# The output products of a state space, two groups of 64 rows in turn, in a hybrid decoder layer

## The chip, the cores and the metric

The kernel runs on one core of one Trainium2 chip. The metric is the device time of one execution in microseconds, lower is better. Times of a kernel are medians of several executions; profiles are of one execution. The engines are named PE (matrix products, with PEld for its weight loads), DVE, ACT, POOL and SP (which issues DMA).

## The reference

One decoder layer over 2048 positions of width 1024, in float32. After an RMSNorm one projection feeds two token mixers: differential attention (4 heads, two softmax maps each) and a diagonal state space of 32 channel groups with 16 channels and 64 complex states each. Both outputs go through one output projection; then come a second RMSNorm, a gated FFN of width 2816, and a last RMSNorm. The part that matters here:

```python
def s5_mixer(u, lam_re, lam_im, log_step, b_re, b_im, c_re, c_im, d, w_glu, b_glu):
    ...
    _, _, x_re, x_im = lax.associative_scan(combine, (a_re, a_im, bu_re, bu_im), axis=1)
    y = (jnp.einsum('ghp,bsgp->bsgh', c_re.astype(f32), x_re)
         - jnp.einsum('ghp,bsgp->bsgh', c_im.astype(f32), x_im)
         + d.astype(f32) * u32)
    y = jax.nn.gelu(y.reshape(bsz, s_len, SSM_WIDTH))
    y = y * jax.nn.sigmoid(y @ w_glu.astype(f32) + b_glu.astype(f32))
    return y.astype(u.dtype)
```

## The kernel before

All matrix products take float32 values split in two parts, a high one and the rest, so each product is three on PE (`mm3`: high by high, high by rest, rest by high).

**The state space** runs in `ssm_pair`, once for each of 16 pairs of channel groups. Positions are cut in 256 blocks of 8. For a pair n the kernel
- loads the inputs u (128 rows for each group), G, H, and every second time T;
- computes the drive z of the states, 6 products of 128 rows by 256 columns into the PSUM tile `pv1` (pv in the profile);
- starts the outputs y with the products of T by u, 3 for each group: group 0 into `fx1` (fx), group 1 into `tp2[1]` (tp);
- copies z to SBUF on ACT, turns and scans it on DVE and POOL, turns it back and splits it into `xh` and `xl`;
- adds the products of H by the states onto the same y. H and the states hold group 0 in rows 0 to 63 and group 1 in rows 64 to 127, so these products have 64 rows. For each group there are 2 halves f of the states by 3 products, 6 in all, 128 by 256 outputs each;
- applies GELU to fx and tp on ACT into `gy` and stores it to `yD`.

In the profile, the products of 64 rows are those of the form `64*128 64x256`, and `pair` is the PSUM of the projections that run between.

**The order of work.** Nothing is issued as it is written. `Rec` records each operation as a task with a cost from a table, and the operands it reads and writes; `Sched` then simulates the engines and writes out an order for each engine's queue, taking of the ready tasks the one with the best priority (`pri`). Operations marked `any` go to DVE or POOL by the plan. Several matrix products in a row become one task: `Rec.call` collects them in `self.open`, and `flush` closes the task, when asked, when the next product writes another PSUM tile, or when the sum of costs passes 1.3. So the six products of group 0 were one task and those of group 1 another, with a `flush` behind each, and the planner could put other work between them. State space tasks have priority -50, and projections of queries, keys and values (-40 and later) fill PE between them. On the chip each engine runs its queue in the planner's order, waiting on semaphores.

**Behind the state space** the last queries and keys (q0, k0) are rotated: ACT copies the projection out of PSUM, PE multiplies it with a permutation (`tp<-misc,cst`), DVE and POOL combine it with cosine and sine, ACT and DVE split it, and SP stores it. It uses buffers of the state space (the tags tr, t1, t2, pq), so it starts when the last pair is done. Then come the last value projections, and `glu`, the gate: it loads `w_glu` in two parts (L1473), splits them (L1479 on ACT, L1480 on DVE or POOL), loads `yD` (L1486), splits it (L1493, L1496), and multiplies (L518 to L520 into fx). The two loads share a ring of three buffers. Attention's score products (L1199) and exponentials (L1237) follow, then output projection and FFN.

Of the kernel before, what the change touches and what calls it, by code (L numbers as in the profile page):

```python
# [167 lines left out]
class Ring:  # L168


    def __init__(self, *tiles):
        self.free = [(0.0, t) for t in tiles]
        self.queues = {}
# [123 lines left out]
class Rec:  # L297


    def __init__(self, S, nc):  # L300
        self.S, self.real, self.pri, self.mem, self.open = S, nc, 0.0, {}, []
        self.areas, self.turned, self.fair = {}, {}, False
        for name, eng in (("vector", "dve"), ("scalar", "act"), ("gpsimd", "pool"), ("tensor", "pe"), ("sync", "sp"),
                          ("any", "any")):
            setattr(self, name, Proxy(self, name, eng))
# [67 lines left out]
    def urgent(self, pri):  # L373
# [4 lines left out]
        self.flush()  # L378
        self.pri = old

    def flush(self):
        if self.open:
            calls, self.open = self.open, []
            self.last = self.task(("pe", sum(c[0] for c in calls)), [("", *c[1:]) for c in calls])

    @staticmethod
    def isap(x):
        return hasattr(x, "tensor") and hasattr(x, "ap")

    def call(self, eng, f, args, kw):  # L390
        isap = self.isap
        outs = [kw[n] for n in ("out", "accum_out") if isap(kw.get(n))]
        rest = [x for n, x in kw.items() if n not in ("out", "accum_out") and isap(x)]
        pos = [x for x in args if isap(x)]
        if "out" not in kw:
            outs.append(pos.pop(0))
        ins = rest + pos
        free = lambda x: math.prod(n for _, n in list(x.ap)[1:])
        n = max([free(outs[0])] + ([free(i) for i in ins] if "reduce" in f else []))
        c = ("", f, outs, ins, args, kw)  # L400
        if eng == "pe":
            cost = n / 2400.0 + 0.0035
            if f == "transpose":
                cost = 0.108
            elif kw["rhs"].dtype == F32:
                cost = max(4 * cost, 0.215)
            if self.open and (sum(x[0] for x in self.open) + cost > 1.3
                              or kw.get("start") and self.where(self.open[-1][2][0]) != self.where(outs[0])
                              or self.open[-1][2][0].tensor.name != outs[0].tensor.name):
                self.flush()  # L410
            self.open.append((cost, f, outs, ins, args, kw))
            return None
        self.flush()
        if f == "dma_start":
            return self.task(("sp", 0.47), [c], size=math.prod(outs[0].shape) * 4)
        psum = [x.space == PSUM for x in (outs[0], *ins)]
        if f == "tensor_tensor_scan" or psum[0]:
            dve = 2.3e-3 * n + 0.03
        elif f in ("tensor_scalar", "memset"):
            dve = 0.75e-3 * n + 0.03  # L420
        else:
            dve = 1.06e-3 * n + 0.06 if any(psum) else 1.27e-3 * n + 0.02
        cost = dict(dve=dve, act=0.87e-3 * n + (0.26 if "accum_out" in kw else 0.08),
                    pool=(1.0e-3 if f == "tensor_scalar" else 0.3e-3 if f == "memset" else 2.0e-3) * n + 0.12)
        if kw.get("op") == ALU.pow:
            cost["pool"] += 0.25 + 0.09 * n
        port = f == "tensor_tensor" and not any(psum)
        if eng == "any":
            return self.task({e: cost[e] for e in ("dve", "pool")}, [c], bias=FAIR if self.fair else BIAS, port=port)
        return self.task((eng, cost[eng]), [c], port=port)  # L430
# [14 lines left out]
def view(t, shape, dt):  # L445

    if dt != F32:
        t = t.bitcast(dt)
    if len(shape) > 2:
        names = "abcdef"[:len(shape) - 1]  # L450
        t = t.rearrange(f"p ({' '.join(names)}) -> p {' '.join(names)}", **dict(zip(names, shape[1:])))
    return t
# [47 lines left out]
class K:  # L500
# [519 lines left out]
    def ssm_pair(self, n):  # L1020

        nc = self.nc
# [8 lines left out]
        G, H = (s3.tile([128, 2, 2, 128], F32R, name="s" + x) for x in "GH")  # L1031
# [33 lines left out]
        y = [z[:, 0:256] for z in (self.fx1, self.tp2[1])]  # L1065
# [6 lines left out]
        lo, hi = slice(0, 64), slice(64, 128)  # L1072
# [10 lines left out]
        r = self.r8[:, n:n + 1].to_broadcast([128, 256])  # L1083
# [9 lines left out]
        v.tensor_tensor(out=t1[:, 1], in0=t1[:, 1], in1=t2[:, 0], op=ALU.add)  # L1093
        xh, xl = (s1.tile(P3, F32R, name=x) for x in ("xh", "xl"))
        self.split(xh[:, :, 1:], xl[:, :, 1:], t1[:, :, 0:255])
        for g in range(2):
            r = slice(64 * g, 64 * g + 64)
            for f in range(2):

                x = f ^ g  # L1100
                self.mm3(y[g], H[r, f, 0], H[r, f, 1], xh[r, x], xl[r, x], False, f == 1, skip_group_check=True)
            nc.flush()
        gy = view(self.gy, P3, F32)
        for g in range(2):
            a_.activation(out=gy[:, g], in_=y[g], func=AF.Gelu_apprx_tanh)
# [1088 lines left out]
```

## Time and profile before

| | |
|---|---|
| Median of three runs | 2430.85 us (2430.6 to 2438.7) |
| The profiled execution | 2428.99 us |
| Its span | 2426.9 us |
| Busy on DVE, ACT, POOL | 67%, 43%, 43% of the span |
| Mean granted clock of PE | 0.985 |
| Moved by DMA | 435.34 MB |

The profile is read from the time of each engine in total to the stages. The work of the state space's pairs lies between 233 and 406 us, the rest of the rotation and of the value projections until about 480 us, attention until about 1150 us, and the FFN fills the rest. In rows of the timeline, the first number is the start in us, the second the time from the first start to the last end, and `x3` says how many instructions were merged; matrix products are pipelined, so the spacing of their starts counts, not their length. Brackets at a row's end give how long the engine sat idle before it, and what ended that.

### The profile page before, as it was taken

What the parts mean: (1) busy time and instruction counts of PE and PEld (TensorE: products, weight loads), DVE (VectorE), ACT (ScalarE), POOL (GpSimd) and SP (SyncE); (2) the same over time, 40 slices, a digit from 0 to 9 for tenths busy, and PEclk for the clock granted to TensorE, in tenths of its full rate; (3) what the DMA queues carried; (4) which work ended last, traced back from release to release, by engine and by line L of the source; (5) the groups of instructions that cost most, each with busy time, mean ns of one, the idle gap of its engine ahead of it and who ended that gap; (6) DMA issues with size and microseconds to landing.
All of it is one profiled execution on the core that took longest, in us unless ns stands there. A gap on an engine that the chain in (4) does not pass through costs nothing.

```text
span 2426.9 us, 34139 instructions
## 1 busy us (share of the span) xinstructions
PE 2335.0 (96%) x11832; PEld 1958.1 (81%) x11832; DVE 1616.7 (67%) x2577; ACT 1048.9 (43%) x2103; POOL 1041.0 (43%) x1048
## 2 busy tenths in 40 slices
PE   7999999989999999998999999999999999999998
PEld 6887797878888888876788888788888878878876
DVE  7885775247887778647877455754544576585698
ACT  7222333247877776545332333533333342242343
POOL 4134675355666556546544322222232223232244
PEclk9999999999999999998999999999999999999999
DMA  6467675665566557787886232532223255575664
GB/s 216 132 191 215 225 220 170 208 215 156 191 199 193 191 187 245 232 294 234 270 285 223 74 97 81 187 109 78 87 72 96 84 165 198 171 256 165 201 201 162
DMA packets 312174, 435.34 MB, mean 179 GB/s; under 512 B 42241, under 2 KB 187713, under 8 KB 312001
## 3 DMA queue, kind: packets, MB, share of 16 engines
q1 hardware_dynamic: 309408, 428.71, 55.4%
q10 hardware_dynamic: 2592, 4.45, 0.5%
q8 instruction: 93, 1.52, 0.3%
q14 instruction: 81, 0.66, 0.1%
HBM read 287.66 MB, written 145.42 MB: 178 GB/s over the span
## 4 chain that ended last, share of the span: by engine, by line
PE 70%; DMA 6%; DVE 4%; issue 3%; POOL 2%; ACT 2%; SPq 0%; POOLq 0%; DVEq 0%; ACTq 0%
PE pair L519 9%; PE pair L520 9%; PE pair L518 9%; PE tp L519 4%; PE tp L520 4%; PE tp L518 4%; PE fx L518 4%; PE fx L519 3%; PE fx L520 3%; PE pv L518 3%; PE pv L519 3%; PE pv L520 3%; PE pair L364 3%; DMA hn<-qD 2%; PE tp L1320 2%
## 5 line engine op out<-in xcount | busy, mean ns | idle before, releaser
L1782 ACT CAST misc<-hn 128x512 fp32r<-128x512 f32 (+1 forms) x340 | 204.8, 609 | 484.2 <-POOL hn L1902 163.0
L519 PE MATMUL pair<-hn,misc 128*128 128x512 f32 x925 | 363.4, 393 | 10.0 <-DVE hn L1783 9.9
L518 PE MATMUL pair<-hn,misc 128*128 128x512 f32 x925 | 362.2, 392 | 0.5 <-ACT misc L1782 0.4
L520 PE MATMUL pair<-hn,misc 128*128 128x512 f32 x925 | 361.9, 391 | 0.2 <-DVE misc L1783 0.2
L1783 DVE TENSOR_TENSOR misc<-hn,misc 128x512 fp32r<-128x512 f32 (+1 forms) x340 | 247.8, 732 | 113.7 <-ACT misc L1782 113.3
L364 PE MATMUL pair<-hn,misc 128*128 128x512 f32 x1152 | 282.8, 399 | 0.0
L364 PEld LDWEIGHTS pair<-hn,misc 128*128 128x128 f32 x1152 | 215.3, 191 | 45.7 <-issue 2.4
L1902 POOL TENSOR_TENSOR hn<-misc,hn 128x512 f32<-128x512 f32 (+1 forms) x68 | 99.9, 1469 | 296.5 <-DVE misc L1783 296.0
L519 PEld LDWEIGHTS pair<-hn,misc 128*128 128x128 f32 x925 | 174.6, 189 | 51.1 <-DVE hn L1783 15.6
L1909 POOL TENSOR_TENSOR hn<-hn 128x512 f32<-128x512 f32 (+1 forms) x68 | 97.1, 1428 | 256.7 <-DVE misc L1783 240.3
L518 PEld LDWEIGHTS pair<-hn,misc 128*128 128x128 f32 x925 | 174.4, 189 | 38.5 <-ACT misc L1782 0.8
L520 PEld LDWEIGHTS pair<-hn,misc 128*128 128x128 f32 x925 | 174.8, 189 | 36.5 <-DVE misc L1783 0.6
L1899 POOL TENSOR_TENSOR misc<-hn 128x512 f32<-128x512 f32 (+1 forms) x68 | 92.9, 1366 | 245.8 <-DVE misc L1783 200.1
L1221 DVE TENSOR_REDUCE small<-pair 128x1 f32<-128x1024 f32 (+7 forms) x160 | 158.2, 992 | 57.3 <-PE pair L1203 27.0
L1237 ACT ACTIVATE hn<-pair,small 128x1024 f32<-128x1024 f32 (+4 forms) x192 | 166.2, 868 | 60.1 <-DVE small L1221 27.1
L519 PE MATMUL tp<-hn,misc 128*128 128x512 f32 x454 | 177.6, 391 | 3.9 <-DVE hn L1783 3.9
L518 PE MATMUL tp<-hn,misc 128*128 128x512 f32 x454 | 177.4, 391 | 2.1 <-ACT misc L1782 1.9
L520 PE MATMUL tp<-hn,misc 128*128 128x512 f32 x454 | 177.2, 390 | 0.0
L364 POOL TENSOR_TENSOR misc<-misc,misc 128x512 f32<-128x512 f32 (+1 forms) x71 | 84.4, 1190 | 162.8 <-DVE misc L364 130.2
L1946 DVE TENSOR_TENSOR misc<-pair,misc 128x512 f32<-128x512 f32 x110 | 75.9, 690 | 95.9 <-PE pair L520 95.6
L364 POOL TENSOR_TENSOR misc<-misc 128x256 f32<-128x256 f32 (+1 forms) x128 | 102.2, 809 | 44.3 <-DVE misc L364 20.0
L364 DVE TENSOR_TENSOR misc<-misc,misc 128x512 f32<-128x512 f32 (+7 forms) x111 | 93.9, 864 | 36.5 <-ACT misc L364 30.5
(268 smaller groups left out, 5724.5 us busy)
## 6 DMA issues: line engine op xcount, KB each, us to landing
hn<-vD SPq DMA_DIRECT2D x48, 512.0 KB
hn<-kD SPq DMA_DIRECT2D x96, 256.0 KB
hn<-in_w_gate SPq DMA_DIRECT2D x44, 512.0 KB
hn<-in_w_up SPq DMA_DIRECT2D x44, 512.0 KB
fD<-misc SPq DMA_DIRECT2D x88, 256.0 KB
misc<-in_w_down SPq DMA_DIRECT2D x77, 256.0 KB
hn<-qD SPq DMA_DIRECT2D x128, 128.0 KB
hD<-misc SPq DMA_DIRECT2D x32, 512.0 KB
```

Source lines behind the costliest of these rows:

```text
L364: getattr(ENGINE[t.at](self.real), f)(*map(now, args), **{n: now(x) for n, x in kw.items()})
L518: nc.tensor.matmul(out, lhsT=ah, rhs=bh, start=start, stop=False, **k)
L519: nc.tensor.matmul(out, lhsT=ah, rhs=bl, start=False, stop=False, **k)
L520: nc.tensor.matmul(out, lhsT=al, rhs=bh, start=False, stop=stop, **k)
L1221: v.tensor_reduce(out=nl[:, i:i + 1], in_=x.got[sc][:, 0:w], axis=AX.X, op=ALU.max, negate=True)
L1237: a_.activation(out=z.got[rings[i]][:, 0:w], in_=x.got[sc][:, 512 * i:512 * i + w], func=AF.Exp, bias=st(n, n + 1), accum_out=acc)
L1782: hf = lambda t: a_.copy(out=dst(t)[0], in_=src())
L1783: lf = lambda t: (g_ if t.at == "pool" else v).tensor_sub(out=dst(t)[1], in0=src(), in1=dst(t)[0].bitcast(F32))
L1899: s1 = any_(n, lambda t, e: e.tensor_tensor(out=t.got[s1r][:, 0:n], in0=q(1, 0), in1=q(1, 1), op=ALU.add), *r, take=[s1r], pri=pri())
L1902: s2 = any_(n, lambda t, e: e.tensor_sub(out=q(0, 0), in0=s1.got[s1r][:, 0:n], in1=q(0, 0)), s1, s3, a11, pri=pri())
L1909: s4 = any_(n, lambda t, e: e.tensor_sub(out=q(0, 1), in0=q(0, 1), in1=q(0, 0)), s2, a12, pri=pri())
L1946: return S("dve", 1.042e-3 * w + 0.07, lambda t: v.tensor_tensor(out=(t if to is None else to).got[tm], in0=x.got[bank], in1=y.got[tm], op ...
```

## The change

In `ssm_pair` the twelve products of H are issued in turn: for each half f and each of the three kinds of product, first group 0 and then group 1. They are the same products, and each group's six are added in the same order. A new `Rec.together` makes one task of all that is issued inside it, and counts each product there at 0.55 of its cost. No other line is changed.

```diff
+    @contextmanager
+    def together(self):
+
+        self.flush()
+        self.joint = True
+        yield
+        self.joint = False
+        self.flush()
...
-            if self.open and (sum(x[0] for x in self.open) + cost > 1.3
+            if self.joint:
+                cost *= 0.55
+            elif self.open and (sum(x[0] for x in self.open) + cost > 1.3
...
-        for g in range(2):
-            r = slice(64 * g, 64 * g + 64)
+
+        with nc.together():
             for f in range(2):
-
-                x = f ^ g
-                self.mm3(y[g], H[r, f, 0], H[r, f, 1], xh[r, x], xl[r, x], False, f == 1, skip_group_check=True)
-            nc.flush()
+                for i, (a, b) in enumerate(((0, xh), (0, xl), (1, xh))):
+                    for g, r in enumerate((lo, hi)):
+
+                        nc.tensor.matmul(y[g], lhsT=H[r, f, a], rhs=b[r, f ^ g], start=False, stop=f == 1 and i == 2,
+                                         skip_group_check=True)
```

The queues change in more places than this, because the planner works with other costs from there on. PE's queue is the same up to the first step of a pair's outputs. There it held, before (misc_1983 holds xh and xl, misc_1976 holds H, pair, hn and misc_118 belong to projections):

```order
L364 MATMUL pair_96<-hn_111,misc_118 128x512
L364 MATMUL pair_96<-hn_110,misc_118 128x512 x2
L364 MATMUL fx<-misc_1983,misc_1976 128x256 x6
L364 MATMUL tp_104<-misc_1983,misc_1976 128x256 x6
L364 MATMUL pair_102<-hn_325,misc_118 128x512
```

and holds now, up to its third product (it goes on so until there are six of each, and then comes the same pair_102):

```order
L364 MATMUL pair_96<-hn_111,misc_118 128x512
L364 MATMUL pair_96<-hn_110,misc_118 128x512 x2
L364 MATMUL fx<-misc_1983,misc_1976 128x256
L364 MATMUL tp_104<-misc_1983,misc_1976 128x256
L364 MATMUL fx<-misc_1983,misc_1976 128x256
```

The twelve products have stayed at their place here, and alternate. In four of the 16 pairs, three products of z (pv) of the next pair stood between the two groups; now nothing does, as it is one task.

The second place is PE's queue behind the last pair, where queries and keys are rotated. Before, ten products of projections or more stood between two rotation products (tp_103 from the table cst), as here:

```order
L364 MATMUL tp_103<-misc_1950,cst 128x512
L364 MATMUL pair_96<-hn_114,misc_118 128x512
L364 MATMUL pair_96<-hn_115,misc_118 128x512
L364 MATMUL pair_96<-hn_114,misc_118 128x512 x2
L364 MATMUL pair_96<-hn_115,misc_118 128x512
L364 MATMUL pair_97<-hn_114,misc_118 128x512
L364 MATMUL pair_97<-hn_115,misc_118 128x512
L364 MATMUL pair_97<-hn_114,misc_118 128x512 x2
L364 MATMUL pair_97<-hn_115,misc_118 128x512
L364 MATMUL tp_103<-misc_1950,cst 128x512
```

Now the first two behind the last step follow each other directly:

```order
L364 MATMUL pair_96<-hn_115,misc_118 128x512
L364 MATMUL pair_96<-hn_114,misc_118 128x512
L364 MATMUL tp_103<-misc_1950,cst 128x512 x2
L364 MATMUL pair_101<-hn_325,misc_118 128x512
L364 MATMUL pair_101<-hn_482,misc_118 128x512
```

Of the projections' products of 512 columns, 96 stood behind the last step, and 71 do now; the other 25 have moved ahead of it.

The third place is SP's queue at the start of the gate. Before, the two parts of w_glu went to two buffers (misc_3765, misc_3828), and the first load of yD to the first of them:

```order
L364 DMA kD<-misc_120 8x16x512
L1473 DMA misc_3765<-in_w_glu 128x1024
L364 DMA kD<-misc_120 8x16x512
L364 DMA qD<-misc_120 128x2x512
L1473 DMA misc_3828<-in_w_glu 128x1024
L364 DMA kD<-misc_120 8x16x512 x2
L1486 DMA misc_3765<-yD 128x4x256
```

Now both parts go to one buffer, and yD to the other:

```order
L364 DMA kD<-misc_120 8x16x512 x2
L1485 DMA misc_3757<-in_w_glu 128x1024
L364 DMA qD<-misc_120 128x2x512
L364 DMA kD<-misc_120 8x16x512 x2
L364 DMA qD<-misc_120 128x2x512
L1485 DMA misc_3757<-in_w_glu 128x1024
L1498 DMA misc_3831<-yD 128x4x256
```

The second part of w_glu has moved behind the use of the first, and the load of yD is free of it. On PE, the first products of the gate now stand behind 120 products of the value projections instead of 144, and 48 more follow behind the first twelve of them; before, they followed behind the first 24.

More of the change, by code (lines that the diff above doesn't have):

```diff
@@ L301, in __init__ @@
         self.S, self.real, self.pri, self.mem, self.open = S, nc, 0.0, {}, []
-        self.areas, self.turned, self.fair = {}, {}, False
+        self.areas, self.turned, self.fair, self.joint = {}, {}, False, False
         for name, eng in (("vector", "dve"), ("scalar", "act"), ("gpsimd", "pool"), ("tensor", "pe"), ("sync", "sp"),
```

## The prediction

> **What bounds the kernel now.** I read the page's busy times first, then the chain that ended last, then the busy time of each engine by stage.
>
> ```profile
> span 2426.9 us, 34139 instructions
> PE 2335.0 (96%) x11832; PEld 1958.1 (81%) x11832; DVE 1616.7 (67%) x2577; ACT 1048.9 (43%) x2103; POOL 1041.0 (43%) x1048
> PE 70%; DMA 6%; DVE 4%; issue 3%; POOL 2%; ACT 2%; SPq 0%; POOLq 0%; DVEq 0%; ACTq 0%
> ...
> core 0: us, PE busy (x) PEld busy (x) DVE busy (x) ACT busy (x) POOL busy (x), PEclk, DMA share, GB/s
> 233.00:406.00 173.00, 167.18 (x1009) 147.52 (x1009) 129.28 (x177) 61.43 (x142) 110.28 (x110) 0.98 0.71 213
> 406.00:440.00 34.00, 33.98 (x158) 26.40 (x158) 12.23 (x16) 10.14 (x18) 22.48 (x17) 1.00 0.48 153
> 480.00:1150.00 670.00, 630.98 (x3896) 542.91 (x3896) 475.12 (x721) 435.59 (x967) 386.13 (x456) 0.97 0.67 212
> ```
>
> PE is busy 96% of the span and is 70% of the last chain, so time taken off PE is worth something where PE does not then wait. The changed products all lie between 249 and 406 us. There PE is busy 167.18 of 173 us, and 33.98 of 34 us just behind. From 480 to 1150 (attention) it is idle 39 us: the stage in which a new order can win or lose most.
>
> **The products as they run now.** The timeline of PE, for the first step of two groups:
>
> ```profile
> 249.01 0.62 PE L364 MATMUL fx<-misc,misc 64*128 64x256 f32 x3
> 249.36 0.38 PE L364 MATMUL tp<-misc,misc 64*128 64x256 f32 x1
> 249.47 0.28 PE L364 MATMUL fx<-misc,misc 64*128 64x256 f32 x1
> 249.58 0.28 PE L364 MATMUL tp<-misc,misc 64*128 64x256 f32 x1
> 249.59 0.28 PE L364 MATMUL fx<-misc,misc 64*128 64x256 f32 x1
> 249.70 0.28 PE L364 MATMUL tp<-misc,misc 64*128 64x256 f32 x1
> 249.71 0.27 PE L364 MATMUL fx<-misc,misc 64*128 64x256 f32 x1
> 249.82 0.52 PE L364 MATMUL tp<-misc,misc 64*128 64x256 f32 x3
> 250.26 1.42 PE L364 MATMUL pair<-hn,misc 128*128 128x512 f32 x5
> ...
> 404.67 0.62 PE L364 MATMUL fx<-misc,misc 64*128 64x256 f32 x3
> ...
> 405.92 7.09 PE L364 MATMUL pair<-hn,misc 128*128 128x512 f32 x30
> ```
>
> The queue holds six fx products, then six tp products, yet the chip already overlaps them: from 249.58 on, one tp and one fx product start 0.01 us apart, and the next two 0.12 us later. So two products of 64 rows in different halves do share a slot of 0.12 us. But this happens only in the middle: three fx products run alone, then a tp and an fx one by themselves, then two shared slots (249.58, 249.70) and three tp products alone. The step takes 250.26 - 249.01 = **1.25 us**, and the last one, 405.92 - 404.67, the same. Twelve of the sixteen steps look like this, these two the first and the last. In the other four, of which the first and the last follow, the planner had put three full-row products between the groups:
>
> ```profile
> 282.59 0.96 PE L364 MATMUL fx<-misc,misc 64*128 64x256 f32 x6
> 283.49 0.62 PE L364 MATMUL pv<-misc 128*128 128x256 f32 x3
> 284.04 0.97 PE L364 MATMUL tp<-misc,misc 64*128 64x256 f32 x6
> 284.94 1.45 PE L364 MATMUL pair<-hn,misc 128*128 128x512 f32 x5
> ...
> 375.51 0.96 PE L364 MATMUL fx<-misc,misc 64*128 64x256 f32 x6
> ```
>
> Here six products alone take 283.49 - 282.59 = 0.90 us, twice, with 0.55 us of pv between.
>
> **What the change removes.** It takes the products in turn, fx, tp, fx, tp, so two neighbours in the queue never use the same half.
> - Price of a new step. From below: six shared slots, the length of one group alone, 0.90 us (six slots of 0.12 us, and 0.2 us for going to half the rows and back). From above: no better than now, 1.25 us. I take **0.90**: the rows at 249.58 and 249.70 show just this pairing, and with neighbours in different halves nothing has to be reached over.
> - Twelve steps: 12 x (1.25 - 0.90) = 4.2 us.
> - Four split steps: 0.90 + 0.90 become 0.90. The pv products between, 0.55 us for three, go back to three plain slots of 0.12 us and lose 0.2 us of switching. 4 x (0.90 + 0.20) = 4.4 us.
> - **PE work saved: 8.6 us**; 3.0 us if the new step stays at 1.25 (only the split ones gain, 4 x (1.80 + 0.20 - 1.25)).
>
> The Trainium skill, page "TensorE: Matmul & The Clock Gate", section "Part 3: Packing small matmuls", states that matmuls start strictly in program order, which would leave the old order no overlap but that of the last fx with the first tp: eleven slots, and the saving would be five slots a step instead of 0.35 us, 11.6 us in all by the slot above. This trace disagrees (a tp product starts at 249.36, before the fourth fx at 249.47, which is ahead of it in the queue), and since the 1.25 us of before are measured, the sum stays at 8.6.
>
> The first group's result used to be read half a step earlier. Now both activations wait for the whole step:
>
> ```profile
> 405.73 0.38 ACT L364 ACTIVATE misc<-fx 128x256 f32<-128x256 f32 x1 [2.13 <-PE fx L364]
> ```
>
> ACT sat idle 2.13 us before it, and it has 111 idle us of 173 in the stage; the output goes to memory and is not read for tens of us. I cost it at nothing; uncovered it would be 0.38 us a step, 6 us in all.
>
> **What it moves.** The planner now sees one task of about 0.73 instead of two of 0.66, so from the first step on every engine's order differs. In PE's queue, 25 more projection products of 512 columns stand ahead of the last step, and 71 instead of 96 behind it, in the stretch in which queries and keys are rotated (tp<-misc,cst):
>
> ```profile
> 412.84 1.02 PE L364 MATMUL tp<-misc,cst 128*128 128x512 f32 x2
> 413.30 2.89 PE L364 MATMUL pair<-hn,misc 128*128 128x512 f32 x10
> 416.02 1.02 PE L364 MATMUL tp<-misc,cst 128*128 128x512 f32 x2
> ```
>
> One projection product takes (412.84 - 405.92)/30 = 0.23 us, so 25 are 5.8 us. The state space thus ends only 8.6 - 5.8 = 2.8 us sooner, and the rotation stretch has 5.8 us less work on PE. If PE sets the stretch, all 8.6 us arrive at its end; if the rotation's own chain over ACT, DVE and POOL sets it, 2.8 us do. PE at 33.98 of 34 us speaks for PE. But two rotation products now stand directly behind one another on one tile; the second must wait until DVE has read the first, where at least 416.02 - 412.84 = 3.18 us lay between two of them so far, of which 0.46 is the product itself (the next row starts at 413.30). That bare wait costs 0 to 2.7 us; I take all of it, as the chain has no other work in it. **Forecast: 8.6 - 2.7 = 5.9 us.** From 480 us on I take the waits to stay as they are, with both signs in the range.
>
> The profiled execution took 2428.99 us (span 2426.9), so it would be 2423.1; the median of the three runs shown is 2430.85, 1.86 above it, and by that **2425.0 us**.
>
> **The rivals.**
> - *The rotation chain takes over, 18%.* Then only 2.8 us arrive: 2428. For it: ACT, DVE and POOL hand the rotation on in steps, and the gate stage behind it is a chain too (below). Against it: PE shows no wait at a rotation product.
> - *The start of the gate stage gets better too, 18%.* PE now waits twice there:
>
> ```profile
> 443.36 7.32 PE L364 MATMUL pair<-misc,hn 128*128 128x256 f32 x48 [3.38 <-DVE misc L364]
> 452.46 7.52 PE L364 MATMUL pair<-misc,hn 128*128 128x256 f32 x48 [1.77 <-DVE misc L364]
> ...
> 442.87 7.64 DMA misc<-yD
> ...
> 450.54 0.70 ACT misc L1493 x2
> ```
>
> The last three lines are the chain: the value projections' split on ACT stands behind a cast (L1493) that waits for yD's load, and SP issued that load into a buffer which the first gate weight had to leave. In the new queue of SP that load goes to another buffer and no longer waits for it. If both waits go, 8.6 + 5.15 = 13.7 us: 2417. Against it: the second gate weight now waits for the first one's split instead, and PE comes to the gate products behind 120 value products instead of 144, with 48 more queued behind them.
> - *Slower: the replanned attention stage waits more, 12%.*
>
> ```profile
> engine line waited for: us in total, times, longest us
> PE pair L1199 <- ACT hn L1237: 8.7, 8, 2.3
> PE pair L1199 <- DMA hn<-qD: 7.3, 6, 2.8
> ```
>
> Score products wait for the exponentials that free their bank, and for queries in flight. If PE arrives sooner while loads and exponentials do not, these 14 waits grow; from 5.9 us on the gain is gone. Doubled, they cost 16.0: 2430.85 - 5.9 + 16.0 = 2441. For it: the planner sees none of the load times that the trace shows. Against it: loads and exponentials are issued behind the same projections, and move with them.
> - *The alternation does nothing, 8%.* The chip overlaps in the old order already; if the new step stays at 1.25 us, 3.0 us remain: 2428.
>
> **How the numbers follow.** Forecast 44%, with 2421 to 2429 as its own range. No single case is bigger. The 80% range leaves out the better part of the gain rival's tail (attention waits falling as well) and the worse half of the slower one: 2411 to 2438. About 0.5% (12 us) is what a measurement of this kernel tells from no change. Faster than 2418.7 are most of the gain rival and a small part of the forecast: 0.20. Slower than 2443 are half of the slower rival and a crumb of the rest: 0.07. Within: 0.73.
>
> **What would show it.** In the profile after: tp and fx rows alternating from the first on, 0.12 us a pair, and 0.9 us from a step's start to the next product (1.25 would be the last rival); no fx group of six followed by pv. PE busy from 233 us to the last step's end down by some 3 us with 25 more projections in it. A wait of PE at the second rotation product of a stretch, under 2.7 us: if several such waits appear, the chain rival. The gate stage's start with its two waits gone, or moved to the gate products. The waits for qD and for L1237 near 16 us: at 30 the slower rival. I would be wrong as a whole if the attention stage's idle 39 us changed by more than 10 either way, since I have no row for the new order there.

## The result: 0.8% slower, and where the profile after shows it

| | us, median (lowest to highest) | ratio to before (95% interval) |
|---|---|---|
| before | 2432.24 (2428.56 to 2438.7), 6 runs | |
| after | 2453.86 (2443.65 to 2456.77), 6 runs | 1.0083 (1.0065 to 1.01) |

The forecast was 2425, the range 2411 to 2438: the sign is wrong, and the time lies outside the range. The profiled execution of the changed kernel took 2455.72 us, its span is 27.0 us longer than that of before.

The head of the page of the changed kernel, and its chain by engine:

```profile
span 2453.9 us, 34165 instructions
PE 2338.9 (95%) x11832; PEld 1956.2 (80%) x11832; DVE 1627.2 (66%) x2580; ACT 1047.8 (43%) x2105; POOL 1042.8 (42%) x1042
PE 80%; DMA 8%; DVE 5%; issue 3%; POOL 2%; ACT 2%; SPq 0%; POOLq 0%; DVEq 0%; ACTq 0%
```

PE runs as many instructions as before, is busy 3.9 us more instead of less, and is idle 23 us more (2453.9 - 2338.9 = 115.0 against 91.9).

The timeline of PE in the changed kernel, the first step and the last:

```profile
250.21 0.38 PE L364 MATMUL fx<-misc,misc 64*128 64x256 f32 x1
250.22 0.38 PE L364 MATMUL tp<-misc,misc 64*128 64x256 f32 x1
250.44 0.28 PE L364 MATMUL fx<-misc,misc 64*128 64x256 f32 x1
250.44 0.28 PE L364 MATMUL tp<-misc,misc 64*128 64x256 f32 x1
...
251.12 1.45 PE L364 MATMUL pair<-hn,misc 128*128 128x512 f32 x5
...
413.66 0.38 PE L364 MATMUL fx<-misc,misc 64*128 64x256 f32 x1
...
414.57 1.66 PE L364 MATMUL pair<-hn,misc 128*128 128x512 f32 x6
```

The pairs start together, from the first on, and a step takes 251.12 - 250.21 = 0.91 us; so does the last. The products themselves do what was forecast. But from the first step's start to the last one's it is now 163.45 us, against 155.66 before (404.67 - 249.01).

The second place is the stretch from the last step to the first load of FFN weights (in_w_gate). Ahead the two loads on SP, then the busy times of that stretch, each first of before, then of the changed kernel:

```profile
1044.14 0.89 SPq L1918 DMA_DIRECT2D hn<-in_w_gate  x2
...
406.00:1044.00 638.00, 606.87 (x3889) 530.10 (x3890) 425.80 (x677) 405.87 (x917) 361.66 (x431) 0.97 0.64 200
```

```profile
1070.24 0.88 SPq L1930 DMA_DIRECT2D hn<-in_w_gate  x2
...
414.00:1070.00 656.00, 609.72 (x3875) 527.38 (x3872) 433.94 (x683) 407.03 (x919) 354.69 (x422) 0.96 0.63 195
```

From the last step's start it was 639.5 us and is 656.6: 17.1 us more. PE's idle time went from 638 - 606.87 = 31.1 to 656 - 609.72 = 46.3 us. PE is also busy 2.9 us longer in it, though 25 products of 0.23 us have moved out of it; by estimate its products ran some 8 us longer, at a lower clock (2.9 + 5.8, less 0.6 of the last step's products that the second window holds; the mean clock is 0.96 against 0.97). So the 27.0 us are 7.8 in the state space's stage, 17.1 in this stretch, 1.2 ahead of the first step, and about 1 behind. Of the 17.1 us, 4.7 lie ahead of the end of the value projections (502.53 us before, 516.20 now), and 12.4 in attention behind it. These are shares of one execution; how far others repeat them stands behind the last experiment.

Which waits, says the list of PE's waits in the two stretches (from the first step on; us in total, times, longest), before (without the two rows that the prediction quotes) and after:

```profile
PE pair L364 <- DVE misc L364: 7.3, 4, 3.4
...
PE pv L364 <- DMA misc<-uD: 4.1, 6, 1.1
...
PE tp L1320 <- DVE hn L1329: 1.4, 2, 0.9
```

```profile
PE pair L1211 <- ACT hn L1249: 12.5, 12, 3.8
PE pair L1211 <- DMA hn<-qD: 8.9, 6, 2.7
PE pv L364 <- DMA misc<-uD: 8.7, 7, 3.4
PE pair L364 <- DVE misc L364: 7.3, 4, 2.1
PE tp L364 <- ACT misc L364: 5.5, 2, 2.8
PE tp L1332 <- DVE hn L1341: 3.7, 4, 2.2
```

(Lines of the changed kernel are up to 12 higher.) No one wait grew much. Exponentials cost 3.8 us more, rotation products 5.5 where they had no wait, loads of u 4.6, transposes behind DVE 2.3, queries 1.6. The gate stage's waits, which one rival wanted gone, total 7.3 us as before.

### The profile page after: what moved, and what is told of

The parts are those of the page before. It is cut to its first block, busy times and chain, and to the rows that moved or that the text cites. A ratio compares the mean times of both kernels' runs of the same rounds, so it can differ in the third digit from the quotient of the medians.

```text
span 2453.9 us, 34165 instructions
## 1 busy us (share of the span) xinstructions
PE 2338.9 (95%) x11832; PEld 1956.2 (80%) x11832; DVE 1627.2 (66%) x2580; ACT 1047.8 (43%) x2105; POOL 1042.8 (42%) x1042
## 4 chain that ended last, share of the span: by engine, by line
PE 80%; DMA 8%; DVE 5%; issue 3%; POOL 2%; ACT 2%; SPq 0%; POOLq 0%; DVEq 0%; ACTq 0%
PE pair L364 12%; PE pair L530 9%; PE pair L531 9%; PE pair L529 9%; PE tp L530 4%; PE tp L531 4%; PE tp L529 4%; PE fx L529 3%; PE pv L529 3%; PE fx L530 3%; PE pv L530 3%; PE fx L531 3%; PE pv L531 3%; PE tp L1332 2%; DMA hn<-qD 2%
## 5 line engine op out<-in xcount | busy, mean ns | idle before, releaser
L364 POOL TENSOR_TENSOR misc<-misc,misc 128x512 f32<-128x512 f32 (+1 forms) x74 | 91.8, 1242 | 163.6 <-DVE misc L364 117.7
```

Source lines behind the costliest of these rows:

```text
L364: getattr(ENGINE[t.at](self.real), f)(*map(now, args), **{n: now(x) for n, x in kw.items()})
```

## The experiments

Two readings were possible. Either the products in turn are good and the planner's new order costs more than they bring; or the products in turn, or the joint task that the GELU must wait for, do harm themselves.

| run | what it is | us | ratio to before |
|---|---|---|---|
| e1 | products in turn, order of before | 2434.22 | 1.0003 (0.9986 to 1.0021) |
| e2 | products not in turn, order of after | 2452.24 | 1.0084 (1.0058 to 1.0111) |
| e3 | changed kernel, planned price 1.0 | 2433.63 | 1.0008 (0.999 to 1.0025) |
| e4 | kernel before, planned price up by 1% | 2455.86 | 1.01 (1.0069 to 1.0132) |
| e5 | changed kernel, gate weights in two buffers | 2452.63 | 1.0085 (1.0061 to 1.0108) |
| e6 | kernel before, gate weights in one buffer | 2449.73 | 1.007 (1.0048 to 1.0092) |
| e7 | changed kernel, planned price 0.69 | 2449.05 | 1.0074 (1.0046 to 1.0101) |
| e8 | changed kernel, planned landing of loads 4.0 | 2473.67 | 1.017 (1.0144 to 1.0197) |
| e9 | two casts behind two exponentials | 2451.39 | 1.0077 (1.006 to 1.0094) |
| e10 | casts and splits behind six exponentials | 2457.86 | 1.0107 (1.0089 to 1.0125) |
| e11 | two rotation products taken apart | 2452.51 | 1.0076 (1.0061 to 1.0091) |
| e12 | e10 and e11 together | 2458.74 | 1.0103 (1.0087 to 1.0119) |
| e13 | changed kernel, planned price 0.98 | 2432.37 | 0.9999 (0.9984 to 1.0015) |
| e14 | changed kernel, planned price 1.05 | 2435.93 | 1.0018 (1.0004 to 1.0032) |
| e15 | changed kernel, planned price 1.10 | 2449.79 | 1.0083 (1.0063 to 1.0104) |

### Turns and order taken apart: e1 to e4

e1 keeps the planner of before, with its two tasks and their prices; when the second group's task comes right behind the first's (12 of 16 steps), the two are written out in turn. The queues of the other four engines are those of before.

```diff
+            if weave and len(weave) == 1:
+                first = weave[0]
...
+                emit([c for p in zip(first, calls) for c in p], eng)
```

> The kernel before, planned as before (two tasks of six products at full cost); only where the two tasks stand next to each other in PE's queue, in 12 of 16 pairs, the twelve products are written out in turn. DVE, ACT, POOL and SP have the queues of before. Theory A (the alternation saves what was forecast, and the loss comes from the new order that the planner draws): steps of 0.91 us instead of 1.25, 3 to 7 us faster than before. Rival B (products in turn are themselves harmful, by the clock or by results that come late): no faster than before, or slower by 10 us and more.

e2 is the changed kernel, one joint task at 0.55, with its products written group by group:

```diff
-            for f in range(2):
-                for i, (a, b) in enumerate(((0, xh), (0, xl), (1, xh))):
-                    for g, r in enumerate((lo, hi)):
+            for g, r in enumerate((lo, hi)):
+                for f in range(2):
+                    for i, (a, b) in enumerate(((0, xh), (0, xl), (1, xh))):
```

> The changed kernel with its plan unchanged (one task at 0.55), but inside the task all six products of group 0 first and then those of group 1, as before. All other queues are those of the changed kernel. Theory A: still some 20 us slower than the kernel before, and a further 2 to 6 us slower than the changed one. Rival B: back to the time before, within 5 us.

e3 and e4 change only a price that the planner reads. In e3:

```diff
-                cost *= 0.55
+                cost *= 1.0
```

> The changed kernel, one task and products in turn, but planned at full cost (factor 1.0 instead of 0.55), so the planner draws a third order. Theory A: the time depends on the order drawn, so it should differ clearly (by 8 us or more) from the changed kernel's, to either side. Rival C (one task instead of two is the harm, since both groups' results come at its end): within 5 us of the changed kernel.

e4 is the kernel before with the products of 64 rows at 1.01 of their price. Every instruction is that of before; only their order can change.

```diff
+            cost *= self.more
...
+        nc.more = 1.01
```

> The kernel before with nothing changed but the planned cost of the 64-row products, by 1 per cent (0.661 to 0.668 for a task). No product is added, removed or turned. Theory A (the order drawn decides, and small causes draw other orders): off the kernel before by 5 us or more to either side, with other waits of PE in attention. Rivals B and C: within 3 us of the kernel before.

e4 decides the larger question: without one product changed, the order that another price makes costs 1.0%. Behind the state space that order is the changed kernel's: planned there, the tasks of PE, ACT, DVE and POOL have the same costs in the same sequence. And e2 shows that the loss stays when the products are not in turn; its steps take 1.25 us again. e1 and e3 have the products in turn and an order behind them that is that of before (e1 word for word, e3 nearly), and cost nothing.

But they bring nothing that can be measured either, at most 3 us (0.9986 is the lower end of e1's interval), which is the other half of the error. In e1 the sixteen steps take 18.27 us instead of 24.01, and from the first product of the first to the last of the last it is 156.3 us, 156.7 before. PE's waits from 240 to 406 us in e1, longer than before where the list has 4.1 and 0.6 in its place:

```profile
PE pv L366 <- DMA misc<-uD: 7.2, 8, 1.6
PE pv L366 <- ACT misc L366: 2.7, 4, 1.2
```

The waits grew by 5 us, about what the steps had saved. The chain of e1 shows one of them (start, length):

```profile
309.13 0.03 PE pv L366
309.16 9.49 DMA misc<-uD
318.65 0.14 issue
318.78 0.59 PE pv L366 x3
```

The load of u is issued when a drive product has released its buffer, and takes 9.5 us; the next drive product waits for its landing. It recurs: five such loads, 43 us, are pieces of e1's chain between 240 and 406 us, and waits for uD total 8.7 us in the changed kernel, 12.4 in e3 and 13.1 in e13, against 4.1 before. So PE's 96.6% did not make it the bound: 5.7 us less work there did not shorten the stage. That the loads and drives set its length instead is a reading of these waits, not shown by a run (e8, below, speaks against so simple a reading).

### Can a single decision be found? e5 to e8

One decision in which the orders part is the gate's weights. In the order of before the two parts go to two buffers, and 144 value products stand ahead of 24 gate products; in the changed kernel both go through one buffer, and value and gate products come in blocks of 48 and 12. e5 gives each part a buffer of its own in the changed kernel; e6 sends both through one in the kernel before.

```diff
+            wr = (w0, w1)[k2]
...
-                in_=A["w_glu"][:, 2 * k2:2 * k2 + 2]), take=[yr], pri=pri(), size=524288)
+                in_=A["w_glu"][:, 2 * k2:2 * k2 + 2]), take=[wr], pri=pri(), size=524288)
```

> The changed kernel; its plan is the same up to the gate's first loads, but the two parts of w_glu must take two different buffers, as they did before. Theory A1 (the 17 us behind the state space hang on the gate's weights passing one after the other through one buffer): 2431 to 2442, that is, 10 to 20 us faster than the changed kernel, with what the state space stage lost (8 us) still lost. Rival A2 (the buffers do not matter; the attention stage's order lost the time): within 5 us of the changed kernel, 2449 to 2459.

In e6 both parts take one ring `wr` of a single buffer:

```diff
-        room(RAW, yr)
+        room(RAW, wr)
...
-                in_=A["w_glu"][:, 2 * k2:2 * k2 + 2]), take=[yr], pri=pri(), size=524288)
+                in_=A["w_glu"][:, 2 * k2:2 * k2 + 2]), take=[wr], pri=pri(), size=524288)
```

> The kernel before; its plan is the same up to the gate's first loads, but both parts of w_glu must pass through one buffer, as in the changed kernel. Theory A1: 10 to 20 us slower than the kernel before. Rival A2: within 5 us of it.

e7 gives the step its measured price, e8 the loads a later landing in the plan, on the thought that a truer planner makes a better order; first the edit of e7, then that of e8, each of the changed kernel:

```diff
-                cost *= 0.55
+                cost *= 0.69
...
-                t.end = self.dma + 1.5
+                t.end = self.dma + 4.0
```

> The changed kernel planned at factor 0.69, which is the step's measured 0.91 us (0.55 plans it at 0.73). The planner again lets both parts of w_glu take one buffer here. Theory A1 (one buffer goes with the slow attention): 2445 to 2460. Rival D (the plan lost because the step was planned too short): within 5 us of the kernel before or faster.

> The changed kernel with the planned time from a transfer's end to its use raised from 1.5 to 4.0 us, nearer to the 6.6 to 8.3 us that loads of u took to land in the trace. Theory E (the state space stage loses what the products save because PE stands at products whose u is still in flight): PE's waits for uD from 240 to 416 us fall from 8.7 to under 3 us, and the time from the first to the last step falls below the 156.7 us of before by 4 us or more. If the planner's landing time is not the cause: waits as they are. The total says little by itself, since the gate's parts again share one buffer and all orders behind differ.

e5 speaks against the buffers as the cause: two buffers, and still slow. e6 is slower as they would have it; but e5, e6 and e8 each redrew everything behind, into a third order. e7 falls into the changed kernel's order and its time. A truer price does not help, and truer landings are worst. But e8 does what it was built for: waits for uD fall from 8.7 to 1.4 us, as expected, and from the first step's start to the last one's it is 152.1 us. It gains nothing by that. The first step starts only at 260.73 us instead of 249.01, and the outputs' products now wait 11.8 us for ACT and DVE (fx, 240 to 416 us), so the last step starts at 412.83 instead of 404.67: with the waits for u nearly gone, the stage does not end sooner. These four leave the cause open.

### Repairing the waits by hand: e9 to e12

The longest wait of the changed kernel. Its ACT timeline and, in the last two rows, PE's:

```profile
663.36 0.37 ACT L1363 COPY hn<-pv 128x256 f32<-128x256 f32 x1 [0.57 <-PE pv L531]
665.77 1.15 ACT L1596 ACTIVATE misc<-misc 128x512 fp32r<-128x512 f32 x2 [2.03 <-DMA misc<-in_w_out]
666.83 1.10 ACT L1249 ACTIVATE hn<-pair,small 128x1024 f32<-128x1024 f32 x1
...
668.07 0.80 PE L1211 MATMUL pair<-hn,hn 128*128 128x512 f32 x1 [3.81 <-ACT hn L1249]
668.66 0.63 PE L1212 MATMUL pair<-hn,hn 128*128 128x512 f32 x1
669.09 0.63 PE L1211 MATMUL pair<-hn,hn 128*128 128x512 f32 x1
```

ACT takes its queue in order, and two casts of output weights (L1596), whose load is in flight, stand ahead of the exponentials that free a score bank. PE waits 3.81 us. Then its products start 0.43 us apart (669.09 - 668.66) instead of 0.23: the busy time by window gives the granted clock as 0.66 between 660 and 690 us:

```profile
660.00:690.00 30.00, 22.07 (x90) 16.83 (x89) 23.23 (x31) 21.96 (x46) 16.89 (x16) 0.66 0.83 268
```

The Trainium skill, page "TensorE: Matmul & The Clock Gate", section "Part 1: The HAM clock gate", says that the array falls to half rate after an idle window of some 3.4 us and is let up again after a busy window of that length. The drop behind 3.81 us of idling agrees; the stay, (1 - 0.66) x 2 x 30 = 20 us, is six such windows long, with further waits of 1.54 and 2.17 us in it. A row of the kernel before does not agree: there the clock fell behind a wait of 1.01 us (last section).

It looked like a place to repair. e9 writes the two casts out behind those two exponentials; the other queues stay.

```diff
-                        a_.activation(out=w[:, i, 0], in_=x.got[ohr][:, 512 * i:512 * i + 512], func=AF.Copy, scale=sc_)
+                        self.behind(c, lambda: a_.activation(out=w[:, i, 0], in_=x.got[ohr][:, 512 * i:512 * i + 512],
+                                                             func=AF.Copy, scale=sc_))
...
+        if c < 2 and self.left > 0:
+            self.late.append(emit)
```

> The changed kernel with one edit of the order: on ScalarE, the first two casts of the output projection's weights, which in the changed kernel stand ahead of two exponentials while their load is still in flight (TensorE then waits 3.8 us at 668 us and runs some 20 us at half its clock), are emitted behind these two exponentials. No other queue changes, and the work is the same. Theory (waits of this kind, made by the redrawn order, and the half clock behind them cost the time): the wait of 3.8 us falls under 1 us, the stretch of half clock behind it goes, and since products start 0.42 instead of 0.23 us apart in it, 20 us at half clock hold some 9 us of loss: 3.8 + 9 is the most, 2441 to 2449 against 2453.9 of the changed kernel, ratio to the kernel before 1.004 to 1.007. Rival (the wait is covered: the work behind it is late in any case, and the loss is spread over many small waits): 2451 to 2457, ratio 1.008 to 1.010, the half clock moves to another place.

The wait went to its neighbours. PE in e9:

```profile
660.33 0.50 PE L1211 MATMUL pair<-hn,hn 128*128 128x512 f32 x1 [3.15 <-ACT hn L1249]
660.67 0.40 PE L1212 MATMUL pair<-hn,hn 128*128 128x512 f32 x1
660.90 0.39 PE L1211 MATMUL pair<-hn,hn 128*128 128x512 f32 x1
...
666.37 0.79 PE L1211 MATMUL pair<-hn,hn 128*128 128x512 f32 x1 [3.75 <-ACT hn L1249]
...
668.66 0.63 PE L1212 MATMUL pair<-hn,hn 128*128 128x512 f32 x1
669.09 0.63 PE L1211 MATMUL pair<-hn,hn 128*128 128x512 f32 x1
```

The exponentials now wait for their maxima on DVE. At the wait of 3.15 us no split stands ahead of these; at that of 3.75 us they stand behind the splits of the same weights. So e10 moves the casts on ACT and the splits on DVE behind six exponentials, as one block. In e10 and e12 this block comes behind the first output products that use these weights: those products do not wait for them, and compute with what stood in the buffers.

```diff
+    late, left = [], 6
...
+        if c in (4,5,6,7) and (self.left > 0 or self.late):
+            self.late.append((tile, emit))
```

> The changed kernel with one edit of the order: the first eight casts (ScalarE) and the first six splits (VectorE) of the output projection's weights, whose loads are in flight when the changed kernel comes to them, are emitted as one block behind six more exponentials and their maxima. The three other queues stay as they are. Moving two casts alone gave 2451.4: the wait went to the exponentials next to them, because the splits still stood ahead of their maxima. Theory (this block in two queues at once makes the three waits of TensorE between 655 and 690 us, 3.8 + 1.5 + 2.2 us, and the 20 us at half clock): waits for exponentials in the whole kernel from 12.5 to 8 or 9 us as in the kernel before (8.7), time 2441 to 2449. Rival (the scores of the longest rows wait there whatever stands in the queue; the kernel before waits 5.8 us at the same place): waits stay at 12 or more, 2450 to 2457.

PE waits 3.15 and 1.20 us there, and then 9.7 us at a transpose, for DVE. There the block's splits wait 5.37 us for its casts on ACT, and these 6.61 us for a load, so the moved block met another load in flight:

```profile
684.65 1.12 PE L1333 MATMUL tp<-cst,hn 128*128 128x128 f32 x4 [9.73 <-DVE hn L1342]
```

The same with the rotation. The changed kernel's second rotation product stands directly behind the first and waits; e11 puts ten projection products between them in PE's queue and changes nothing else.

```diff
+                    turns and Rec.since < 9:
+                Rec.held.append((*mine, lambda at=t.at: emit(at)))
+                return
```

> The changed kernel with one edit of TensorE's queue alone: where two rotation products stand directly behind one another, the second is emitted ten projection products later, and each of the following rotation products as the next one falls due, so that they stand as far apart as in the kernel before. All other queues stay. Theory (the bare rotation product costs what was priced, 2.7 us, and half clock behind it): the wait of 2.68 us falls under 0.5, last step to last value product 97 to 99 us instead of 101.7 to 104.5 in the runs with this order; the time falls by 3 to 4 us, to 2448 to 2452, which 5 rounds hardly tell from 2453.9. Rival (the chain over ScalarE, VectorE and GpSimd sets the stretch): the wait turns up at the next rotation or value product, 101 to 104 us, no change of time.

Two rows of PE in the changed kernel, then the same place in e11:

```profile
420.25 1.12 PE L364 MATMUL tp<-misc,cst 128*128 128x512 f32 x2 [0.16 <-DVE misc L364]
424.05 2.07 PE L364 MATMUL tp<-misc,cst 128*128 128x512 f32 x2 [2.68 <-ACT misc L364]
```

```profile
418.24 1.12 PE L374 MATMUL tp<-misc,cst 128*128 128x512 f32 x2 [0.17 <-DVE misc L374]
422.05 3.75 PE L374 MATMUL pair<-hn,misc 128*128 128x512 f32 x10 [2.69 <-ACT misc L374]
```

The wait is the same to 0.01 us, now at a projection product: what is late is an activation on ACT that copies a projection out of PSUM, and both products wait for it. The neighbourhood of the two rotation products had no part in it. e12 does both repairs, with the edits of e10 and e11 in one kernel:

> Both repairs at once (the block of casts and splits behind six exponentials, the rotation products apart) in the changed kernel. Theory (the loss is the sum of such places): 2437 to 2446, and waits for exponentials and rotation together 6 to 9 us less than in the changed kernel. Rival (TensorE gives back at the next place what it gains at one): 2449 to 2457.

All four miss their theory. PE gets back at the next place what it is given at one, because what it waits for (in e11 an activation, in e9 maxima, in e10 a block behind a load) comes no earlier.

### The order as a whole: e13 to e15

If no single place holds the loss, the order as a whole may. Planned without running, 19 prices between 0.40 and 1.15 fall into two orders of the work behind the state space: that of the changed kernel for 14 (0.40 to 0.95, and 1.10), that of before, or nearly, for five (0.98, 1.0, 1.02, 1.05, 1.15). The border is not monotonic, so price and order can be told apart with one number in one line:

```diff
-                cost *= 0.55
+                cost *= 0.98
```

> The changed kernel with the planned price of the step's products at 0.98 of the full price instead of 0.55; the instructions are the same, and only the planner's order differs. Its order behind the state space is that of the kernel before (the two parts of the gate's weights through two buffers, 144 value products in one run, then 24 gate products). Theory (two orders exist, and the one that the planner falls into decides the time, not the price that it is given): 2428 to 2439, ratio 0.998 to 1.003, no wait of 2.7 us at a rotation product. Rival (a price nearer to the truth, 0.7, makes the better order, or the order decides nothing): at a price so far off, as slow as the changed kernel or slower, 2449 or more.

In e14 the number is 1.05, in e15 1.10.

> The same with the price at 1.05. Its order is the one of the kernel before again. Theory (the order decides): 2428 to 2439. Rival (the price decides, the further off the slower): above 2449.

> The same with the price at 1.10. Five hundredths more, and the planner falls back into the changed kernel's order (both parts of the gate's weights through one buffer, 12 and 48 products in turn). Theory (the order decides): 2447 to 2457, ratio 1.006 to 1.010, two waits of 2.7 us at rotation products, 12 to 14 us for exponentials. Rival (prices at and above 1 are as good as that of the kernel before): 2428 to 2439.

e13 and e14 are as fast as before within 0.2%, e15 is slow. Their lists of PE's waits, e13 and then e15:

```profile
PE pair L1211 <- ACT hn L1249: 8.3, 8, 1.9
PE tp L1332 <- DVE hn L1341: 1.4, 2, 0.9
PE tp L364 <- ACT misc L364: 0.5, 1, 0.5
```

```profile
PE pair L1211 <- ACT hn L1249: 12.8, 13, 3.6
PE tp L1332 <- DVE hn L1341: 4.5, 4, 2.9
PE tp L364 <- ACT misc L364: 2.8, 1, 2.8
```

The stretch from the last step to the FFN's weights, in e13 and in e15:

```profile
407.00:1043.00 636.00, 602.81 (x3891) 526.06 (x3891) 427.86 (x677) 405.97 (x917) 362.13 (x432) 0.98 0.64 201
```

```profile
410.00:1062.00 652.00, 607.42 (x3884) 526.34 (x3885) 434.90 (x683) 406.41 (x919) 354.50 (x422) 0.98 0.64 196
```

33.2 us idle of 636 in the one, 44.6 of 652 in the other, as 31.1 of 638 before and 46.3 of 656 in the changed kernel. The same instructions, and a price 0.05 apart from e14: the order decides, and it makes 14 us against e14 and 17 against e13. One expectation missed in detail: e15 has one rotation wait of 2.8 us, not two.

The profiles of all runs say which share of the loss is the order's. From the last step's start to the first load of in_w_gate, the five with the order of before (before, e1, e3, e13, e14) take 637 to 641 us, the nine with the changed one (after, e2, e4, e7, e9 to e12, e15) 653 to 661. From the first step to the last it is 155.6 to 158.0 and 156.1 to 165.3. The changed kernel's 7.8 us in that stage are no fixed price: e9, whose PE has the same queue up to there, takes 157.9 us, with a mean clock of 0.98 in the stage where the changed kernel's profile has 0.95. The loss that repeats is the one behind the last step.

And the planner itself had part of it. Run alone, it plans the start of the last task at 2332.5 us for the kernel before and between 2333.1 and 2336.3 for the five prices with its order, but at 2343.6 for the changed kernel, between 2342.5 and 2346.0 for all 14 prices with that order, and at 2346.9 for e4. So some 11 us of the loss stood in the plan before anything ran on the chip: the planner chooses task by task, and nothing compares the ends of two plans.

## Why the prediction was wrong

- **The new step, 0.90 us: right.** 0.91 measured. All sixteen together, from each one's first product to the next other work, went from 24.01 to 17.44 us: 6.6 saved, where the prediction's 8.6 hold 7.8 for the same stretches (0.8 are for pv's switching). Some products of a few steps still wait (two steps took 1.44 and 3.12 us).
- **"If PE sets the stretch, all 8.6 us arrive at its end; ... PE at 33.98 of 34 us speaks for PE": the first step that failed.** e1 saves 5.7 us in the steps and nothing measurable in the time. That PE was 97% busy did not make it the bound: the planner had laid projections into its gaps, and that work was there to be moved. In e1 the waits for u and for ACT grew by 5.2 us instead. The row of 4.1 us waits for uD, by far the largest in the stage, pointed at loads of u; whether they alone set the stage stays open, as e8 nearly ended these waits and the stage did not end sooner.
- **25 more projection products ahead of the last step: right** in number. They add 5.8 us of work where the steps saved 6.6, and the stage did not get the 2.8 us shorter that were forecast; no run with the changed order has it shorter than the 155.7 us of before.
- **The bare rotation product, 2.7 us: right in size, wrong in cause and count.** It came twice (2.68 and 2.79). e11 shows that the projections between were not the cover: the late activation is what PE waits for. By the prediction's own sign, several such waits speak for the rival in which the rotation's chain takes over.
- **"From 480 us on I take the waits to stay as they are": the step that cost the sign.** The order there was redrawn, and attention, behind the value projections, is 12.4 of the 27 us; together with the rotation and the values, which were to cost 2.7 us and have 5.8 us less work, the stretch is 17.1. e4 and e15 show that this has nothing to do with the products. The prediction had no row for the new order there and said so, and gave the slower case 12% all the same; the planner's own two ends, 11 us apart, would have been one.
- **The slower rival** had the right kind of mechanism, and its size came out smaller: the waits for exponentials and queries went from 16.0 to 21.4 us, not to 32. The rest came from waits that it did not name, and from the half clock behind the longest of them. Its reason is not quite so: the planner does book loads, only with a landing of 1.5 us, which e8 raised to 4.0 without a gain.
- **The gate's start, and the GELU behind the whole step:** the gate's waits neither went nor grew. The later GELU cost nothing that shows: e3 and e13 have it and lose nothing.

Open is which decision of the new order costs. Three repairs moved waits about; two buffers did not bring the old order back. None of the fifteen kernels beats the one before by a measurable amount.

## What to carry to other kernels

Where a planner sets the queues, an edit has two effects, the work that it saves and the redraw, and the second can be larger: change one price by 1% with the work untouched, and the spread that this gives is the least that a forecast's range must hold. Where the planner simulates the engines, compare its ends for both orders first: here they were 11 us apart, with the right sign. Take the edit alone, in the old order, to see what it is worth. An engine that is busy 97% of a stage with work that could also stand elsewhere need not be its bound; look for the chain that would remain with that work gone. And a wait repaired by hand is no gain until what it waits for comes earlier.

## What was not expected of the hardware

Half clock cannot be told from the length of one wait. In e9 products of 512 columns start 0.23 us apart behind a wait of 3.15 us (660.90 - 660.67), and 0.43 apart behind one of 3.75 (669.09 - 668.66). That looks like a border between the two, but in the kernel before the clock falls to 0.50 at 256 us, with no wait over 1.01 us in the 16 us ahead of it (rows of PE, then the busy time by window):

```profile
252.69 0.59 PE L364 MATMUL pv<-misc 128*128 128x256 f32 x3 [1.01 <-DMA misc<-uD]
254.16 0.59 PE L364 MATMUL pv<-misc 128*128 128x256 f32 x3 [0.17 <-DMA misc<-uD]
...
254.00:255.00 1.00, 0.83 (x5) 0.87 (x6) 0.74 (x1) 0.15 (x1) 0.92 (x2) 1.00 0.52 201
256.00:257.00 1.00, 1.00 (x3) 0.78 (x3) 0.97 (x2) 0.62 (x1) 0.92 (x2) 0.50 0.82 254
```

In the changed kernel the wait of 3.81 us was followed by some 20 us at half clock; in e9, with the same order on four engines, the granted clock from 640 to 720 us was 0.96, where the changed kernel had 0.87. What decides between such cases, no run here shows.
